# Retention projection of a decoder trunk: two heads as seven block products and two plain, or all four heads as seven block products with gates kept on the chip

## The chip, the core and the metric

The kernel runs on one core of one Trainium2 chip. Five engines with instruction streams of their own work side by side: TensorE (PE, with its weight loads as PEld), VectorE (DVE), ScalarE (ACT), GpSimd (POOL) and SyncE (SP). Each takes its instructions in the order in which they were written into its stream; semaphores hold an instruction until what it reads is there. Here SP and POOL mostly issue transfers between DRAM and SBUF. The metric is the device time of one execution in microseconds (us). All data are float32.

## The reference, cut to what matters

Two layers (DEPTH = 2) run over 512 tokens of width 1024. Each has a mixer (dilated attention beside retention), a residual with LayerNorm, and a SwiGLU feed-forward part. The change is in the mixer, from the point where both branches are there:

```
# _hybrid_mixer; y_a: 512 x 384 (attention), y_b: 512 x 2048 (retention, 4 heads x 512)
merged = (sigmoid(gate_a) * (y_a @ w_attn_proj)      # 384 x 1024
        + sigmoid(gate_b) * (y_b @ w_ret_proj))      # 2048 x 1024
return merged @ w_out                                # 1024 x 1024
```

`y_b @ w_ret_proj` is the **retention projection**, `y_a @ w_attn_proj` the attention projection, `merged @ w_out` the output projection.

## The kernel before

**Precision.** A float32 operand is split into a high and a low half of a shorter type (`hilo`): ACT casts the high half (L95), DVE subtracts it from the source for the low half (L96). A product is three matmuls (`mm3`): high by high, high by low, low by high. A matmul here takes a 128x128 token piece against 512 columns of weights, so a triple belongs to one k tile (128 rows of the weights) and one token tile (128 tokens). A `unit` is the split of one loaded 128x1024 weight tile: one cast, one subtraction. Its results come from pools of 4 `whi` and 4 `wlo` tiles; loaded tiles (`raw`) come from a pool of 8.

**Seven block products.** Where a product is written as 2 by 2 blocks, seven block products take the place of eight (`ORDER`, L313): A11·B11, A12·B21, S1·P1, S4·B22, S2·P2, S3·P3, A22·P4. A is the left side (tokens by k; first index the token half, second the k half), B the weights (k half, column half). The sums are S1 = A21−A22, S3 = A11−A21, S2 = S1−A11, S4 = S2+A12 on the left, and P1 = B11+B12, P2 = P1+B22, P4 = P2+B21, P3 = B12+B22 on the right. Some products add up in one PSUM pair (`CHAIN`), the rest is put together from PSUM by DVE.

**The mixer's end, in order of time** (in layer 0; layer 1 repeats it):

1. *Gates.* `gates(c)` computes the sigmoid gates. The attention gate stays in SBUF (`sga`), the retention gate goes from `sb` to DRAM (`g_d[1]`, L1113). The retention output y_b, transposed, is in DRAM (`y_d`). Near the end of the gates `y_blocks` loads four y blocks of heads 0 and 1 (`yr`, 128x4x256, L1092) on SP's queue.
2. *Attention projection* (L1145 to L1156): eight groups of nine matmuls. After each, DVE multiplies the gate by the product (L1153, 128x512) and POOL writes the result to `g_d[0]` (L1154). Between them stand ACT's and DVE's halves of y: `y_put` splits a block into `xh`, `xl`; `x_sums` (L213) forms S1, S3, S2, S4 on DVE and splits them into `xs`.
3. *Retention projection*: k tiles 0 to 7 (heads 0, 1) as seven block products (`product`: 7 x 4 k tiles x 2 token tiles), k tiles 8 to 15 (heads 2, 3) plainly (`plain`: 8 x 4 x 2 column halves). The seven products are interleaved with the two plain column halves. The weight sums grow in two tiles `p1`: SP loads B11, and POOL issues **adding DMAs** (transfers that add DRAM rows to what stands in SBUF; L1218) for B12, B22 and B21. A further pair gets B12 from SP and B22 by adding DMA (L1331). `yq_load` and `yq_put` bring the y of heads 2 and 3 (`yp`).
4. *Merging.* As results come out of PSUM, `gated` loads both gate products from `g_d` (512 KB each time), multiplies (L1252), adds (L1253), and puts a `turn` into the queue of side operations: four PE transposes (`px`, L1260), split into `m`.
5. *Output projection*, residual, norm.

**What sets the order.** The program is written in one order. Side operations stand in a list (`side`); `tick` pops one from it after so many microseconds' worth of matmuls. Within an engine the order is then fixed.

Of the kernel before, what the change touches and what calls it, by code (L numbers as in the profile page):

```python
# [55 lines left out]
def hybrid_kernel(ctx, tc, x, rel_bias, w_in, b_in, w_attn_proj, w_ret_proj, w_out,  # L56
# [457 lines left out]
    g_d = drp.tile([2, S, D], F32, name="g_d")  # L514
# [169 lines left out]
    def layer(ly, cp):  # L684
# [311 lines left out]
        with ret:  # L996
# [82 lines left out]
            sbp, sbs, yrs = [rp, 2], [], ExitStack()  # L1079
# [4 lines left out]

            def y_blocks():
                yas.close()
                ret.close()
                sbp[:] = lay.enter_context(stage("sbp")), 4
# [5 lines left out]
            def y_put(a, b):  # L1094
                ks, ts_ = slice(4 * b, 4 * b + 4), slice(a * 256, a * 256 + 256)
                hilo(yb[a][b], xh[:, ks, ts_], xl[:, ks, ts_])

            def gates(c):
# [10 lines left out]
                def right(i, t):  # L1109
                    sb = sbp[0].tile([P, S], F32, tag="sb", name="sb", bufs=sbp[1])  # L1110
                    sbs.append(sb)
                    act.activation(out=sb, in_=t, func=AF.Sigmoid)
                    act.dma_start(g_d[1, i * P:(i + 1) * P, cs], sb)  # L1113
# [11 lines left out]
            act.copy(out=xh[:, 0:8:4, 0:1], in_=sbs[-3][:, 0:2].unsqueeze(2))  # L1125

            def block_w(b, u):
                k = 4 * (b[1] == "2") + 2 * u
                c = (b[2] == "2") * S
                return wr_l[:, k:k + 2, c:c + S]  # L1130

            def plain_w(u, hf):
                return wr_l[:, 2 * RH + 2 * u:2 * RH + 2 * u + 2, hf * S:(hf + 1) * S]
# [25 lines left out]
        yrs.close()  # L1159

        fin = ExitStack()
        fp = fin.enter_context(stage("fin", side="right"))
        xt = [fp.tile([P, 2, D], F32, name="xtok")]
        res = (x if ly == 0 else spill).rearrange("(h i p) d -> h p i d", p=P, h=2)

# [34 lines left out]
        with stage("mp") as mp:  # L1200

            m = mp.tile([P, 2, KD, S], F32R, name="m")
            turns = [0] * NI
            rate[0], credit[0] = 0.5 / STEP, 0.0
            with stage("yp") as ypp, stage("pp", side="right") as ppp:
                pt = ppp.tile([P, 2, 2, S], F32, name="p1")
                p1 = [pt[:, u] for u in range(2)]
                yp = ypp.tile([P, 2, 6, S], F32R, name="yp")

                def y_tok(k, i):  # L1210
                    if k < 6:
                        return (yp[:, e, k, i * P:(i + 1) * P] for e in range(2))
                    ks, o = 2 * (k - 6) + i // 2, 256 + i % 2 * P
                    return (t[:, ks, o:o + P] for t in (xh, xl))

                def p_load(u, b, add):
                    if add:
                        pool.dma_start(p1[u], block_w(b, u), accum_op=ALU.add)  # L1218
                    else:
                        nc.sync.dma_start(p1[u], block_w(b, u))  # L1220

                def p_units():
                    return [unit(p1[u]) for u in range(2)]

                def product(an, units, pss, fresh):
                    ks = [(u, k) for u in units for k in range(2)]
                    for a in range(2):
                        for j, ((h, l), k) in enumerate(ks):
                            ah, al = x_left(an, j, slice(a * P, (a + 1) * P))
                            mm(pss[a], ah, h[:, k], fresh and j == 0, False)  # L1230
                            mm(pss[a], ah, l[:, k], False, False)
                            mm(pss[a], al, h[:, k], False, j == len(ks) - 1)
                            tick(STEP)

                def plain(u, unit_, pss):
                    h, l = unit_
                    for k in range(2):
                        for i in range(NI):
                            yh, yl = y_tok(2 * u + k, i)
                            mm(pss[i], yh, h[:, k], i >= 2 and u == 0 and k == 0, False)  # L1240
                            mm(pss[i], yh, l[:, k], False, False)
                            mm(pss[i], yl, h[:, k], False, u == 3 and k == 1)
                            tick(STEP)

                gv = {}

                def g_load(i, hf):
                    gv[i, hf] = load(g_d[:, i * P:(i + 1) * P, hf * S:(hf + 1) * S].rearrange("b p c -> p b c"), 2, S)

                def gated(i, hf, v):  # L1250
                    g = gv[i, hf]
                    dve.tensor_tensor(out=g[:, 1], in0=g[:, 1], in1=v, op=ALU.mult)  # L1252
                    dve.tensor_tensor(out=g[:, 0], in0=g[:, 0], in1=g[:, 1], op=ALU.add)  # L1253
                    turns[i] += 1

                    def turn():
                        turns[i] -= 1
                        px = psum()
                        for d in range(4):
                            pe.transpose(px[:, d * P:(d + 1) * P], g[:, 0, d * P:(d + 1) * P], ident)  # L1260
                        ks, ts_ = slice(4 * hf, 4 * hf + 4), slice(i * P, (i + 1) * P)
                        hilo(px.rearrange("p (d t) -> p d t", d=4), m[:, 0, ks, ts_], m[:, 1, ks, ts_])

                    side.extend([nothing] * (i % 2 == 0) * 2 + [turn])

                def pair():
                    return [psum("ps") for _ in range(2)]

                def copies(pss):
                    ts = [work("sn") for _ in pss]  # L1270
                    for t, ps in zip(ts, pss):
                        act.copy(out=t, in_=ps)
# [74 lines left out]
                for i in (2, 3):  # L1347
                    g_load(i, 1)
# [248 lines left out]
```

## Time and profile before

| what | value |
|---|---|
| median of 3 runs | 2100.8 us (2099.79 to 2102.8) |
| the profiled execution | 2106.83 us |
| its span (first to last instruction) | 2105.1 us, 33783 instructions |
| matmul records | 13178 |
| adding DMAs of L1218 and L1331, both layers | 16 |

The page gives busy time by engine, 40 slices of the span, the queues, the chain of work that ended last, and the costliest groups of instructions. A timeline row reads: start, duration, engine, line, operation, output <- inputs, shape; in brackets the idle time before it and what ended that. The durations of successive DVE or ACT rows overlap by a few hundredths, so what one instruction costs in a row of many is read from start to start. In layer 0 the attention projection's matmuls begin at 566.18 us and end at 582.50; the retention projection begins there and ends about 668.75. Layer 1 does the same 1043.5 us later (its attention projection begins at 1609.72 us).

### The profile page before, as it was taken

How to read it: one execution, taken by the hardware profiler on the slowest of the kernel's cores; microseconds unless marked ns; L12 is line 12 of the kernel's file. 1: busy time of each engine (PE TensorE's matmuls, PEld its weight loads, DVE VectorE, ACT ScalarE, POOL GpSimd, SP SyncE). 2: the span in 40 equal slices, each digit the busy share in tenths (PEclk: the TensorE clock that was granted, in tenths of full speed). 3: DMA queues.
4: the chain of work that ended last, by engine and by line, in shares of the span. 5: the costliest groups of instructions: out<-in, count | busy, mean ns of one | idle time of the engine just before them, and what ended most of it. 6: DMA issues, size and time to landing. Idle time of an engine off the chain costs nothing.

```text
span 2105.1 us, 33783 instructions
## 1 busy us (share of the span) xinstructions
PE 2084.9 (99%) x13178; PEld 1863.1 (89%) x13178; DVE 1622.4 (77%) x2327; ACT 1127.8 (54%) x1727; POOL 279.9 (13%) x288
## 2 busy tenths in 40 slices
PE   9999999999999999999999999999999999999998
PEld 8989888888878898999899898888888789989897
DVE  7666898786766698887787578887868577988876
ACT  5567655655643365555355766555656334655551
POOL 3111111110010101111030111111100111110101
PEclk9999999999999999999999999999999999999999
DMA  8866557676898458868258554758767973687771
GB/s 241 209 173 139 141 143 193 166 178 161 256 276 250 89 150 205 192 156 229 81 156 225 140 140 122 196 140 210 182 161 257 271 235 72 173 197 179 191 195 45
DMA packets 303553, 374.38 MB, mean 178 GB/s; under 512 B 22941, under 2 KB 208441, under 8 KB 303264
## 3 DMA queue, kind: packets, MB, share of 16 engines
q1 hardware_dynamic: 213056, 259.30, 40.0%
q0 software_dynamic: 62928, 100.11, 25.4%
q10 hardware_dynamic: 27408, 12.80, 2.1%
q8 instruction: 103, 1.69, 0.3%
q14 instruction: 58, 0.48, 0.1%
HBM read 346.30 MB, written 28.53 MB: 178 GB/s over the span
## 4 chain that ended last, share of the span: by engine, by line
PE 83%; DVE 5%; issue 5%; DMA 4%; ACT 2%; POOL 1%; ACTq 0%; SPq 0%; POOLq 0%; DVEq 0%
PE ps L84 74%; PE px L84 6%; DMA p<-in_w_ret_proj 2%; DMA raw<-in_w_in 1%; DVE wlo L351 1%; PE px L582 1%; ACT whi L345 1%; PE px L1044 1%; DVE wlo L96 1%; PE px L193 1%; DMA g_d<-sb 1%; DVE xs L96 0%; DVE sg L1153 0%; DVE yr L213 0%; PE px L1260 0%
## 5 line engine op out<-in xcount | busy, mean ns | idle before, releaser
L351 DVE TENSOR_TENSOR wlo<-raw,whi 128x1024 fp32r<-128x1024 f32 (+1 forms) x518 | 605.2, 1172 | 202.7 <-ACT whi L345 187.2
L345 ACT CAST whi<-raw 128x1024 fp32r<-128x1024 f32 (+1 forms) x518 | 519.5, 1007 | 451.0 <-PE ps L84 191.3
L84 PE MATMUL ps<-xs,whi 128*128 128x256 f32 x2176 | 399.5, 284 | 0.4 <-ACT sn L814 0.3
L84 PE MATMUL ps<-whi,xs 128*128 128x512 f32 (+1 forms) x1152 | 348.0, 372 | 2.1 <-ACT sn L496 2.1
L84 PEld LDWEIGHTS ps<-xs,whi 128*128 128x128 f32 x2176 | 339.5, 192 | 4.9 <-issue 1.7
L84 PE MATMUL ps<-xh,whi 128*128 128x256 f32 (+1 forms) x1104 | 318.3, 290 | 1.7 <-ACT xh L95 1.4
L84 PE MATMUL ps<-xl,whi 128*128 128x256 f32 (+1 forms) x1104 | 315.5, 286 | 0.0
L84 PE MATMUL ps<-xh,wlo 128*128 128x256 f32 (+1 forms) x1104 | 315.0, 286 | 0.0
L84 PE MATMUL ps<-xs,wlo 128*128 128x256 f32 x1088 | 308.0, 283 | 1.2 <-DVE wlo L351 1.2
L84 PEld LDWEIGHTS ps<-whi,xs 128*128 128x128 f32 x1152 | 210.0, 188 | 36.6 <-ACT sn L496 2.6
L84 PEld LDWEIGHTS ps<-xh,whi 128*128 128x128 f32 x1104 | 210.4, 191 | 9.6 <-ACT xh L95 2.8
L84 PEld LDWEIGHTS ps<-xl,whi 128*128 128x128 f32 x1104 | 211.4, 192 | 3.0 <-DVE xl L96 0.6
L84 PE MATMUL ps<-wlo,xs 128*128 128x512 f32 (+1 forms) x576 | 213.5, 371 | 0.4 <-DVE wlo L96 0.2
L84 PEld LDWEIGHTS ps<-xh,wlo 128*128 128x128 f32 x1104 | 211.2, 191 | 1.5
L84 PEld LDWEIGHTS ps<-xs,wlo 128*128 128x128 f32 x1088 | 208.5, 192 | 1.8 <-DVE wlo L351 1.8
L336 POOL DMA_DIRECT2D raw<-in_w_in x80 | 97.3, 1238 | 696.5 <-DMA raw<-in_w_in 204.8
L367 DVE TENSOR_TENSOR raw<-raw 128x1024 f32<-128x1024 f32 (+1 forms) x148 | 173.9, 1175 | 10.5 <-DMA raw<-in_w_in 8.5
L84 PE MATMUL ps<-whi,xh 128*128 128x512 f32 (+1 forms) x464 | 174.4, 376 | 0.0
L84 PE MATMUL ps<-whi,xl 128*128 128x512 f32 (+1 forms) x464 | 171.9, 370 | 0.0
L84 PE MATMUL ps<-wlo,xh 128*128 128x512 f32 (+1 forms) x464 | 171.8, 370 | 0.0
L84 PE MATMUL ps<-whi,ht 128*128 128x512 f32 x544 | 170.1, 390 | 0.0
L95 ACT CAST whi<-raw 128x1024 fp32r<-128x1024 f32 (+1 forms) x78 | 76.0, 984 | 100.5 <-PE ps L84 57.4
(247 smaller groups left out, 3307.7 us busy)
## 6 DMA issues: line engine op xcount, KB each, us to landing
raw<-in_w_in SPq DMA_DIRECT2D x168, 512.0 KB, 5.2
raw<-in_w_in POOLq DMA_DIRECT2D x64, 512.0 KB, 8.7
raw<-in_w_ffn_up SPq DMA_DIRECT2D x64, 512.0 KB, 5.0
raw<-in_w_ffn_down SPq DMA_DIRECT2D x52, 512.0 KB, 4.7
raw<-in_w_ffn_gate SPq DMA_DIRECT2D x44, 512.0 KB, 4.8
raw<-in_w_ffn_gate POOLq DMA_DIRECT2D x40, 512.0 KB, 7.3
raw<-in_w_ret_proj SPq DMA_DIRECT2D x32, 512.0 KB, 8.2
raw<-in_w_in SPq DMA_DIRECT2D x56, 256.0 KB, 4.9
```

The lines of the kernel that those rows point to most:

```text
L84: pe.matmul(ps, lhsT=a, rhs=b, start=start, stop=stop, skip_group_check=True)
L95: act.copy(out=hi, in_=src)
L96: dve.tensor_tensor(out=lo, in0=src, in1=hi.bitcast(F32), op=ALU.subtract)
L193: pe.transpose(px[:, d * P:(d + 1) * P], src[:, (4 * hf + d) * P:(4 * hf + d + 1) * P], ident)
L336: pool.dma_start(r, self.src({"P1": "B12", "P3": "B22"}[n], u), accum_op=ALU.add)
L345: act.copy(out=h, in_=src)
L351: dve.tensor_tensor(out=l, in0=src, in1=h.bitcast(F32), op=ALU.subtract)
L367: dve.tensor_tensor(out=r, in0=r, in1=self.t["B22" if n == "P2" else "B21", u], op=ALU.add)
L582: pe.transpose(px[:, hh, j * P:(j + 1) * P], ss[od][:, hh, j * P:(j + 1) * P], ident)
L1044: pe.transpose(px[:, t * P:(t + 1) * P], ys[i][:, t * P:(t + 1) * P], ident)
```

## The change

All 16 k tiles are now one set of seven block products: a block is 8 k tiles by 512 columns, in four units of two k tiles. The stream has 28 steps (`n`), four to a product (`g = n // 4`), each with 12 matmuls; `emit(n)` issues the conversion of a unit two steps ahead, and, behind it, the adding DMA or the load that follows in the same tile.

- **Weights.** Four raw tiles `pch` hold B11 and turn into P1, P2 and P4 in place by adding DMAs on POOL's queue (`add`, L1148). `b21` are loaded ahead; `b22` are loaded while product 1 (A12·B21) runs, and get B12 added in the tile (P3) once S4·B22 has used them. Per layer that is 16 adding DMAs on weights, where there were 8.
- **y.** Eight `yr` tiles, two to a block (L1097). S1 overwrites A22 (L1151), S3 overwrites A21 (L1155), S2 overwrites S1 (L1158). S4 = S2+A12 is formed by an adding DMA that adds A12 from DRAM to the tile of S2 (L1166, POOL's queue, two of them). A22 is loaded again into the tile of S3 (L1170, SP).
- **Gates.** The products of the attention gate stay in SBUF; the writes L1154 are gone, `g_d` holds the retention gate alone, and `gated` loads 256 KB each time. The sums go through `sga` (L1251).
- **Order.** Ahead of the first transposes stand four empty side operations (two before). Both `xtok` loads and the parameters of the norm are issued behind the last adding DMA on POOL.

The core of the diff, with the functions that the change adds:

```diff
@@ y blocks, attention projection
-                for a, b in ((0, 0), (0, 1), (1, 1), (1, 0)):
-                    yb[a][b] = yr.tile([P, 4, 256], F32, name=f"yr{a}{b}")
-                    nc.sync.dma_start(yb[a][b], y_v[:, 4 * b:4 * b + 4, a * 256:a * 256 + 256])
+                for a, b in ((0, 0), (1, 0), (1, 1), (0, 1)):
+                    yb[a][b] = [yr.tile([P, 4, 256], F32, tag=f"yr{a}{b}{u}", name="yr") for u in range(2)]
+                    for u in range(2):
+                        nc.sync.dma_start(yb[a][b][u], y_part(a, b, u))
...
-            b11, b21 = ([load(block_w(n, u), 2, S) for u in range(2)] for n in ("B11", "B21"))
-            for b in range(2):
-                y_put(0, b)
-            s1, s3, s2, s4 = x_sums(yb)
-            more = [lambda: y_put(1, 1), s1, s3, s2]
+            pch = [load(block_w("B11", u), 2, S) for u in range(4)]
+            b21 = [load(block_w("B21", u), 2, S) for u in range(4)]
+            def add(r, b, u):
+                pool.dma_start(r, block_w(b, u), accum_op=ALU.add)
+            def s1(u):
+                dve.scalar_tensor_tensor(out=a22[u], in0=a21[u], scalar=one, in1=a22[u], op0=ALU.mult, op1=ALU.subtract)
+                hilo(a22[u], xs[:, u, 0], xs[:, u, 1])
+            def s3_raw(u):
+                dve.tensor_tensor(out=a21[u], in0=a11[u], in1=a21[u], op=ALU.subtract)
+            def s2_raw(u):
+                dve.tensor_tensor(out=a22[u], in0=a22[u], in1=a11[u], op=ALU.subtract)
+            def s2_put(u):
+                for q in range(2):
+                    t = slot("s2")
+                    s2.append(t)
+                    h, l = (t[:, e].rearrange("p (k t) -> p k t", k=2) for e in range(2))
+                    hilo(a22[u][:, 2 * q:2 * q + 2], h, l)
+                pool.dma_start(a22[u], y_part(0, 1, u), accum_op=ALU.add)
+            def s3_put(u):
+                y_put(0, u, a21[u])
+                nc.sync.dma_start(a21[u], y_part(1, 1, u))
+            def s4_put(u):
+                hilo(a22[u], xs[:, 2 + u, 0], xs[:, 2 + u, 1])
+            for u in range(2):
+                y_put(0, u, a11[u])
+            for u in range(2):
+                y_put(256, u, a12[u])
+            more = [lambda f=f, u=u: f(u) for f in (s1, s3_raw, s2_raw, s2_put) for u in range(2)]
+            more += [nothing] * 2 + [lambda f=f, u=u: f(u) for f in (s3_put, s4_put) for u in range(2)]
+            more += [lambda u=u: y_put(256, u, a21[u]) for u in range(2)]
+            def emit(n):
+                g, u = divmod(n, 4)
+                if g in (0, 2, 4, 6):
+                    stream.append(unit(pch[u]))
+                    if g < 6:
+                        add(pch[u], ("B12", "B22", "B21")[g // 2], u)
+                elif g == 1:
+                    stream.append(unit(b21[u]))
+                    b22.append(load(block_w("B22", u), 2, S))
+                elif g in (3, 5):
+                    stream.append(unit(b22[u]))
+                    if g == 3:
+                        add(b22[u], "B12", u)
+                else:
+                    stream.append(unit(wo[u]))
+                if g in (5, 6):
+                    wo.append(load(wo_l[:, 2 * u:2 * u + 2, (g - 5) * S:(g - 4) * S], 2, S))
             for hf in range(2):
-                if hf:
-                    u11 = [unit(r) for r in b11]
                 for i in range(NI):
...
                     dve.tensor_tensor(out=v, in0=v, in1=ps, op=ALU.mult)
-                    pool.dma_start(g_d[0, i * P:(i + 1) * P, hf * S:(hf + 1) * S], v)
-                    if hf * NI + i >= 2 and more:
+                    if hf * NI + i >= 2:
                         more.pop(0)()
-            s4()
+                    if hf * NI + i in (5, 7):
+                        emit(len(stream))
@@ the stream (products and plain halves before)
+            for n in range(28):
+                g, u = divmod(n, 4)
+                i, an, _ = ORDER[g]
+                c = CHAIN[i]
+                emit(n + 2)
+                if more:
+                    more.pop(0)()
...
+                for k in range(2):
+                    for a in range(2):
+                        ah, al = y_left(an, 2 * u + k, slice(a * P, (a + 1) * P))
+                        p_ = pss[c][a]
+                        mm(p_, ah, h[:, k], i in FIRST and u == 0 and k == 0, False)
+                        mm(p_, ah, l[:, k], False, False)
+                        mm(p_, al, h[:, k], False, u == 3 and k == 1)
+                        tick(STEP)
```

The order of instructions shows three places. The first is DVE, from its first gate product to the low half of the first weight unit of A11·B11 (`wlo` of 128x1024, in the last row); `xl` and `xs` are low halves of y blocks and of their sums, the number behind a name tells buffers apart. Before:

```order
L1153 TENSOR_TENSOR sg_5355<-sg_5355,ps_6006 128x512
L96 TENSOR_TENSOR xl_80<-yr11_5883,xh_79 128x4x256
L1153 TENSOR_TENSOR sg_5386<-sg_5386,ps_6018 128x512
L213 TENSOR_TENSOR yr11_5883<-yr10_5885,yr11_5883 128x1024
L1153 TENSOR_TENSOR sg_5616<-sg_5616,ps_6030 128x512
L213 TENSOR_TENSOR yr10_5885<-yr00_5879,yr10_5885 128x1024
L96 TENSOR_TENSOR xs_81<-yr11_5883,xs_81 128x1024
L1153 TENSOR_TENSOR sg_5638<-sg_5638,ps_6044 128x512
L96 TENSOR_TENSOR wlo_6060<-raw_5994,whi_6059 128x1024
```

In the changed kernel the same stretch of DVE begins with a gate product, a first L1151 and a second gate product, and goes on:

```order
L1151 SCALAR_TENSOR_TENSOR yr_5888<-yr_5884,one_5979,yr_5888 128x1024
L1223 TENSOR_TENSOR sg_5616<-sg_5616,ps_6051 128x512
L96 TENSOR_TENSOR xl_80<-yr_5891,xh_79 128x4x256
L96 TENSOR_TENSOR xl_80<-yr_5892,xh_79 128x4x256
L96 TENSOR_TENSOR xs_81<-yr_5887,xs_81 128x1024
L1223 TENSOR_TENSOR sg_5638<-sg_5638,ps_6065 128x512
L96 TENSOR_TENSOR xs_81<-yr_5888,xs_81 128x1024
L1223 TENSOR_TENSOR sg_5355<-sg_5355,ps_6079 128x512
L1155 TENSOR_TENSOR yr_5883<-yr_5879,yr_5883 128x1024
L1223 TENSOR_TENSOR sg_5386<-sg_5386,ps_6091 128x512
L1155 TENSOR_TENSOR yr_5884<-yr_5880,yr_5884 128x1024
L96 TENSOR_TENSOR wlo_6104<-raw_6005,whi_6103 128x1024
```

Ahead of the first weight unit stood four gate products and four operations of 128x1024 before; now six gate products and eight operations of 128x1024 stand there. Between this unit and the second one stand two more gate products and two L1158 now, nothing before.

The second place is ACT in the products A11·B11 and A12·B21 of the changed kernel: `whi` are the high halves of weight units (the last two those of P1, from `raw_6005` and `raw_6007`), `xs` the high halves of S4, `sn` copies of the first product.

```order
L95 CAST whi_6227<-raw_6017 128x1024
L95 CAST xs_81<-yr_5887 128x1024
L1267 COPY sn_6223<-ps_6149 128x512
L1267 COPY sn_6224<-ps_6150 128x512
L95 CAST whi_6253<-raw_6019 128x1024
L95 CAST xh_79<-yr_5884 128x4x256
L95 CAST whi_6274<-raw_6005 128x1024
L95 CAST xs_81<-yr_5888 128x1024
L95 CAST whi_6297<-raw_6007 128x1024
```

Before, ACT had there:

```order
L95 CAST whi_6193<-raw_6149 128x1024
L95 CAST xs_81<-yr11_5883 128x1024
L1272 COPY sn_6198<-ps_6164 128x512
L95 CAST whi_6233<-raw_6231 128x1024
L95 CAST yp_6146<-raw_6151 128x1024
L95 CAST yp_6146<-raw_6229 128x1024
L95 CAST whi_6267<-raw_6265 128x1024
```

Both have a cast of S4 into `xs` ahead of weight units; now there are two of them, and what they read (`yr_5887`, `yr_5888`) is written by adding DMAs instead of by DVE.

The third place is POOL's transfers in this part of a layer. Before:

```order
L1154 DMA g_d<-sg 128x512 x8
L1342 DMA xtok<-in_x 128x2x1024
L1218 DMA p_6145<-in_w_ret_proj 128x2x512 x4
L1331 DMA raw<-in_w_ret_proj 128x2x512 x2
L1218 DMA p_6145<-in_w_ret_proj 128x2x512 x2
```

In the changed kernel:

```order
L1148 DMA raw<-in_w_ret_proj 128x2x512 x3
L1166 DMA yr<-y_d 128x4x256
L1148 DMA raw<-in_w_ret_proj 128x2x512
L1166 DMA yr<-y_d 128x4x256
L1148 DMA raw<-in_w_ret_proj 128x2x512 x12
L1329 DMA xtok<-in_x 128x2x1024 x2
```

The eight writes are gone, eight adding DMAs on weights and two on y have come, and the two on y stand behind three and four on weights.

More of the change, by code (lines that the diff above doesn't have):

```diff
@@ L1124, in layer @@
             drain()
-            act.copy(out=xh[:, 0:8:4, 0:1], in_=sbs[-3][:, 0:2].unsqueeze(2))
+            late = sbs[-3]
+            act.copy(out=xh[:, 0:8:4, 0:1], in_=late[:, 0:2].unsqueeze(2))
+            act.copy(out=xh[:, 0, 256:257], in_=late[:, 0:1])
+            one = sm.tile([P, 1], F32, tag="one", name="one", bufs=1)
+            dve.tensor_scalar(one, late[:, 0:1], 0.0, 1.0, op0=ALU.mult, op1=ALU.add)
             def block_w(b, u):
-                k = 4 * (b[1] == "2") + 2 * u
+                k = 8 * (b[1] == "2") + 2 * u
@@ new lines, in layer @@
+            for u in range(2):
[5 more added lines that the diff above has]
+            more += [lambda u=u: y_put(256, u, a21[u]) for u in range(2)]
+            wo_l = rows(w_out[ly])
+            b22, wo, stream = [], [], []
+            def emit(n):
[15 more added lines that the diff above has]
+                    wo.append(load(wo_l[:, 2 * u:2 * u + 2, (g - 5) * S:(g - 4) * S], 2, S))
@@ new lines, in layer, with g_load, g_slot, g_small @@
+            gv = {}
+            def g_load(hf, pair, ts):
+                for i, t in zip(pair, ts):
+                    gv[i, hf] = t
+                    nc.sync.dma_start(t, g_d[i * P:(i + 1) * P, hf * S:(hf + 1) * S])
+            def g_slot():
+                t = slot("gb", F32)
+                return [t[:, q] for q in range(2)]
+            def g_small():
+                return [sbp[0].tile([P, S], F32, tag="sb", name="gb", bufs=2) for _ in range(2)]
+            def gated(i, hf, v, o_=None):
+                g, ga = gv[i, hf], sga[i][:, hf]
+                if o_ is None:
+                    o_ = ga
+                dve.tensor_tensor(out=g, in0=g, in1=v, op=ALU.mult)
+                dve.tensor_tensor(out=o_, in0=ga, in1=g, op=ALU.add)
+                turns[i] += 1
+                def turn():
+                    turns[i] -= 1
+                    px = psum()
+                    for d in range(4):
+                        pe.transpose(px[:, d * P:(d + 1) * P], o_[:, d * P:(d + 1) * P], ident)
+                    ts_ = slice(i * P, (i + 1) * P)
+                    hilo(px.rearrange("p (d t) -> p d t", d=4), m[hf][:, 0, :, ts_], m[hf][:, 1, :, ts_])
+                side.extend([nothing] * (1 if i % 2 else 4) + [turn])
@@ L1158, in layer @@
+            emit(30)
+            emit(31)
         lay.close()
[L1159 removed]
         fin = ExitStack()
[L1162 to L1163 removed]
+        fp = fin.enter_context(stage("fin"))
+        xt = [fp.tile([P, 2, D], F32, tag=f"xtok{n}", name="xtok") for n in range(2)]
         res = (x if ly == 0 else spill).rearrange("(h i p) d -> h p i d", p=P, h=2)
+        for t, src in zip(xt, res):
+            pool.dma_start(t, src)
@@ new lines, in layer, with m_tok, evo @@
+        with stage("lp") as lp:
+            xc = [[lp.tile([P, 4, 256], F32, name=f"xc{a}{b}") for b in range(2)] for a in range(2)]
+            ln_par(lp.tile([P, 2 * D], F32, name="lnp"), ln1_g[ly], ln1_b[ly])
+            def m_tok(k, i):
+                return (m[k // 4][:, e, k % 4, i * P:(i + 1) * P] for e in range(2))
+            def evo(hf, i, ps):
+                residual(i, hf, ps, True, True)
+                if hf == 1:
+                    norm(i)
+                    side.extend([nothing] * (6, 2, 5, 4)[i] + to_xT(xtok(i), i, xc))
+            units = [stream[28:], tail_units(wo[4:])]
+            for hf, toks in ((0, (0, 1)), (1, (0,)), (1, (1,)), (0, (2, 3)), (1, (2,)), (1, (3,))):
+                while any(turns[i] for i in toks):
+                    side.popleft()()
+                xstat(units[hf], S, m_tok, lambda i, ps, hf=hf: evo(hf, i, ps), toks=toks)
```

241 lines of the change are left out of this document (66 added, 175 removed).

## Prediction

> **What bounds the kernel now.** I read the page's share of the engines first, then its chain of work that ended last, then the stretch that the change touches, by windows.
>
> ```profile
> PE 2084.9 (99%) x13178; PEld 1863.1 (89%) x13178; DVE 1622.4 (77%) x2327; ACT 1127.8 (54%) x1727; POOL 279.9 (13%) x288
> PE 83%; DVE 5%; issue 5%; DMA 4%; ACT 2%; POOL 1%; ACTq 0%; SPq 0%; POOLq 0%; DVEq 0%
> 566.18:582.50 16.32, 16.32 (x73) 13.51 (x72) 15.51 (x18) 8.63 (x11) 2.90 (x6) 1.00 0.92 335
> 582.50:593.38 10.88, 10.88 (x49) 9.01 (x48) 10.88 (x11) 10.30 (x13) 2.22 (x4) 1.00 0.78 265
> 593.38:640.00 46.62, 45.25 (x203) 36.88 (x202) 21.38 (x23) 14.23 (x19) 8.41 (x8) 1.00 1.00 276
> 640.00:668.75 28.75, 28.75 (x136) 23.75 (x135) 19.56 (x26) 10.87 (x13) 3.05 (x4) 1.00 0.74 218
> PE px L1260 <- DVE raw L1253: 1.3, 1, 1.3
> ```
>
> TensorE is the bound: busy 99% of the span. The windows are the attention projection, the first product A11·B11, and two pieces of the rest of the retention projection (columns: PE, PEld, DVE, ACT, POOL busy us with instructions, granted clock, DMA share, GB/s). The clock is 1.00 in all of them. But TensorE's margin is thin in its helpers: DVE has 15.51 of 16.32 us in the attention projection and all of 10.88 us in the first product, and the DMA engines are full (1.00) from 593.38 to 640.00. The last row (PE's waits between 550 and 740 us: total, times, longest) is the only wait of size there: 1.3 us for the first transposes. So fewer matmuls shorten the time one for one, and every us by which DVE or a transfer comes late lengthens it.
>
> **The matmuls removed.** The timeline of PE around 582 us:
>
> ```profile
> 582.50 0.39 PE L84 MATMUL ps<-whi,xh 128*128 128x512 f32 x1
> 582.73 0.39 PE L84 MATMUL ps<-wlo,xh 128*128 128x512 f32 x1
> 582.95 0.39 PE L84 MATMUL ps<-whi,xl 128*128 128x512 f32 x1
> ```
>
> One matmul costs 0.227 us (0.68 for a triple, start to start). Before, a layer has 7·4·2 triples for heads 0 and 1 and 8·4·2 for heads 2 and 3, 120 in all; now 7·8·2 = 112. 24 matmuls go: 24 x 0.227 = **−5.4 us per layer**, all on the path. The wait for the first transposes goes too, since four empty side operations stand ahead of them now: **−1.4** (the 1.3 above and about 0.1 behind it; if the copy of the other pair is late as well, 0).
>
> **What DVE must do before the first product.** Its timeline in the attention projection:
>
> ```profile
> 570.49 0.68 DVE L1153 TENSOR_TENSOR sg<-sg,ps 128x512 f32<-128x512 f32 x1
> 571.09 1.22 DVE L96 TENSOR_TENSOR xl<-yr,xh 128x1024 fp32r<-128x1024 f32 x1
> 572.22 0.68 DVE L1153 TENSOR_TENSOR sg<-sg,ps 128x512 f32<-128x512 f32 x1
> 572.82 1.22 DVE L213 TENSOR_TENSOR yr<-yr,yr 128x1024 f32<-128x1024 f32 x1
> 573.96 0.68 DVE L1153 TENSOR_TENSOR sg<-sg,ps 128x512 f32<-128x512 f32 x1
> L1183 DVE SCALAR_TENSOR_TENSOR xtok<-xtok,mv,lnp x16: 1272/1276/1278, 688.6 to 2098.1; 128x1024 f32<-128x1024 f32 x16
> ```
>
> Start to start a gate product costs 0.60 and any 128x1024 operation 1.14. (S1 is now a scalar_tensor_tensor; the nearest row is L1183 with 1.276 for the same size against 1.22, so I take the same.) From 570.49 on, the order has six gate products and eight operations of 128x1024 ahead of the first low half: 6·0.60 + 8·1.14 = 12.7 us, then 1.22 for itself. The eight y tiles are eight transfers of 0.524 MB; at the 335 GB/s of the first window that is 1.6 us each. The first landed when ACT's first `xh` started:
>
> ```profile
> 564.50 1.05 ACT L95 CAST xh<-yr 128x1024 fp32r<-128x1024 f32 x1 [2.82 <-DMA yr<-y_d]
> ```
>
> From there the eighth (A12) comes at 564.5 + 7·1.57 = 575.5, so A12's low halves hold DVE by about 1.1 us. The low half is there at 570.49 + 12.7 + 1.1 + 1.2 = 585.5; PE asks for it at 582.95 (two high products first). **+2.6** (with no wait for y and with 2.5 us of it: 1.5 and 4). Between this unit and the next stand two gate products and two operations of 128x1024: 585.5 + 2·0.60 + 2·1.14 + 1.2 = 590.1. PE has 14 matmuls to run by then, to 588.7: **+1.4** (0 to 2.1; nothing if ACT and DVE gain what they wait before). Before, the same work lay beside 192 plain matmuls and cost nothing.
>
> **S4 by an adding DMA.** This is the new wait. What an adding DMA takes here: the line that issues them, the timeline of ACT, and the queues between 613 and 623 us (packets, MB, share of 16 engines):
>
> ```profile
> DMA to landing us min/median/max: 5.5/7.6/11.7
> 610.56 1.05 ACT L95 CAST whi<-p 128x1024 fp32r<-128x1024 f32 x1 [15.27 <-DMA p<-in_w_ret_proj]
> 616.48 1.06 ACT L1272 COPY sn<-ps 128x512 f32<-128x512 f32 x2
> q0 software_dynamic: 536, 1.03, 67.5%
> q1 hardware_dynamic: 430, 0.83, 23.8%
> 601.30 1.23 POOL L1218 DMA_DIRECT2D p<-in_w_ret_proj  x1 [7.90 <-DMA p<-in_w_ret_proj]
> ```
>
> q0 is POOL's queue. Its 1.03 MB, two adds, had 67.5% of the 16 engines for 10 us: 3.4 us of all engines for each (a plain load of the same size: 23.8% of 10 us for 0.83 MB, 1.5 us). Issuing costs POOL 1.2 us. The adds on y have 1 KB rows, half as long as those on weights; no row shows that form, so I bound it by the weights' 3.4 below and, doubled with the rows, 6.8 above, and take 4.0, near the row. The first add on y can be issued when S2's halves are out and the third weight add is: about 592.5. The weight adds are issued as their tiles have been split, at 585.5, 590.2 and 591.4; queued one after another they land near 593, 596 and 599.4, and the y add, with loads of b22 beside it, at 604.2, 11.7 us after issue, which is the longest that the row above shows.
>
> [...]
>
> Behind the cast of S4 on ACT stand two copies of the first product and the last unit of B21, then the cast of P1's first unit. From 604.2: cast 1.05, copies 1.06, cast of the unit 1.05, its low half on DVE 1.2: 608.5. PE reaches that unit 68 matmuls after 590.1, at 605.5, and has one high product to run: **+2.8** (0 to 6: 0 where the add lands by 601.4, up to 8.9 us after issue, 6 where the longer form holds). The second add on y has one weight add ahead of it: at 4.0 each it lands at 612.3; cast of S4, cast and low half of P1's second unit, 615.8. PE comes there 24 matmuls after 608.5, at 614.0: **+1.8** (0 to 4). Then PE's first transposes, four empty operations behind the gated sums, want two gated results that DVE can make only behind the delayed low halves: five 128x512 and two 128x1024, 5.3 us after 615.8, at 621.1, against 619.5 by PE: **+1.6** (0 to 2).
>
> **What I cost at nothing.** The sixteen weight adds: each is issued eight steps (8·2.72 = 21.8 us) before its use. Four make 4·3.4 = 13.6 us of engine time per product of 10.9 us in the first three adding groups, so the cover shrinks by 3 us per group but does not run out (if it does: rival three). The eight writes that go and the halved gate loads free transfers that nobody waited for. The loads of w_out, `xtok` and the norm's parameters now come earlier or beside 20 us of matmuls. Six more weight units (28 for 22) and the extra y halves fill DVE where the third and fourth windows show it half to two thirds busy.
>
> **Sum.** Per layer −5.4 − 1.4 + 2.6 + 1.4 + 2.8 + 1.8 + 1.6 = +3.4; both layers have the same order, so **+6.8**. Against the profiled 2106.83 us (span 2105.1 and 1.7 around it) that is 2113.6; the profiled execution stands 6.0 above the median of the runs, so the runs' median would be 2100.8 + 6.8 = **2107.6 us**.
>
> **The rivals.**
>
> *The y adds land in time* (the other side: faster). Deciding point: an add lands by 601.4, at most 8.9 us after issue. The median of 7.6 speaks for it; that three weight adds stand ahead in the same queue speaks against. Then 2.8 and 1.8 go and 1.6 shrinks to about 0.4: −6.8 + 4.0 + 0.4 = −2.4 per layer, 2096. With DVE's lower bounds (1.5 and 0) it would be 2091.
>
> *Only one of the two adds is late.* Per layer −6.8 + 4.0 + 2 to 3 = about 0: 2101 to 2103.
>
> *The adds fall behind PE.* Twenty-eight steps last 76 us; sixteen weight adds and two on y take 18·3.4 = 61 us of all engines, the twelve plain loads of b22, wo 12·1.5 = 18: 79 us in all. If the queue does not run ahead at the start, PE waits in P2 and P4 too, by some 5 to 9 us per layer: 2118 to 2126. For it speaks that the DMA engines were full for 46 us before, with half the adds; against it that the writes are gone, and the loads of B11 and B21 are done before the stream.
>
> **How the numbers follow.** Forecast 0.44, y adds in time 0.28, one late 0.14, adds fall behind 0.14. The range takes most of the first rival and half of the last: 2093 to 2121. A measurement of this kernel can tell about 0.2% (4.2 us) from no change: faster is below 2096.6, slower above 2105.0. Faster: somewhat over half of the first rival and little else, 0.20. Same: the rest of it, the second, and the forecast's low end, 0.34. Slower: 0.46.
>
> **What would show it.** In the profile after: 48 fewer matmuls; PE idle some 2.6 us before the second matmul of A11·B11, released by DVE `wlo`; ACT's `xs` cast waiting for a DMA on `yr` from `y_d`, and PE some 23 us into the projection waiting for a `whi` or `wlo` behind it; the y add's time to landing near 11 us. No such wait of ACT, or adds that land in under 9 us, would make the first rival true; waits for weight units in the last four products would make the third true. The prediction would be wrong altogether if DVE were found to run ahead in the attention projection by starting S1 earlier, or if POOL issued its adds later than reckoned.

## The result, and the profile after

| | us |
|---|---|
| before, median of 6 runs | 2102.4 (2099.8 to 2104.5) |
| changed, median of 6 runs | 2119.9 (2116.6 to 2122.8) |
| ratio, 95% interval | 1.0084 (1.0071 to 1.0097) |
| profiled execution, span | 2121.81, 2120.0 |

The change costs 17.5 us. The forecast was slower by 6.8, with a range from 2093 to 2121: the direction held, and the time lies near the range's upper end; the size forecast was less than half. First the page and TensorE's four longest waits between 550 and 740 us (total, times, longest) in the changed kernel, then windows of layer 0 from the first matmul of the attention projection to the first of the output projection (columns as before).

```profile
PE 2083.3 (98%) x13130; PEld 1855.4 (88%) x13130; DVE 1644.6 (78%) x2347; ACT 1146.2 (54%) x1747; POOL 297.2 (14%) x292
PE 82%; issue 8%; DMA 3%; DVE 3%; ACT 2%; POOL 1%; ACTq 0%; POOLq 0%; DVEq 0%
PE ps L84 <- DVE wlo L96: 3.5, 2, 2.6
PE ps L84 <- DVE sn L1314: 3.0, 1, 3.0
PE ps L84 <- ACT whi L95: 2.0, 2, 1.3
PE px L1258 <- DVE sg L1251: 1.1, 1, 1.1
566.71:583.03 16.32, 16.32 (x74) 13.52 (x73) 14.01 (x15) 9.15 (x11) 0.00 (x0) 1.00 1.06 374
583.03:593.91 10.88, 7.60 (x25) 5.49 (x24) 10.88 (x13) 4.78 (x7) 3.96 (x4) 0.84 0.54 114
593.91:640.53 46.62, 42.94 (x188) 34.07 (x187) 32.02 (x33) 23.82 (x27) 16.71 (x14) 1.00 1.10 230
640.53:677.77 37.24, 34.28 (x150) 27.50 (x149) 27.80 (x32) 18.75 (x21) 1.20 (x1) 0.95 0.87 246
```

The 48 matmuls are gone (13178 to 13130). In the four windows that the forecast shows for the same stages TensorE was busy through 101.20 of 102.57 us; now it is busy through 101.14 of 111.06. It pauses in three of four windows, and in two of them the granted clock is below 1 (0.84 and 0.95). Where the time went is best read as the length of the retention projection, from the start of the attention projection's last matmul to that of the output projection's first: 86.5 us in layer 0 and 86.6 in layer 1 before, **95.0 and 91.9** now (582.80 to 677.77 and 1634.85 to 1726.73), 13.7 us more in all. The spans differ by 14.9; the remaining 1.2 lies outside these two stretches.

The pauses one by one, on the engines that end them. In the timelines of DVE and of ACT in the changed kernel:

```profile
582.10 1.22 DVE L1155 TENSOR_TENSOR yr<-yr 128x1024 f32<-128x1024 f32 x1
583.24 0.68 DVE L1223 TENSOR_TENSOR sg<-sg,ps 128x512 f32<-128x512 f32 x1
583.83 1.22 DVE L1155 TENSOR_TENSOR yr<-yr 128x1024 f32<-128x1024 f32 x1
584.97 1.22 DVE L96 TENSOR_TENSOR wlo<-raw,whi 128x1024 fp32r<-128x1024 f32 x1
603.77 1.05 ACT L95 CAST xs<-yr 128x1024 fp32r<-128x1024 f32 x1 [5.40 <-DMA yr<-y_d]
612.79 1.05 ACT L95 CAST xs<-yr 128x1024 fp32r<-128x1024 f32 x1 [4.16 <-DMA yr<-y_d]
660.56 1.05 ACT L95 CAST xs<-raw 128x1024 fp32r<-128x1024 f32 x1 [1.43 <-DMA raw<-in_w_out]
661.64 1.23 DVE L96 TENSOR_TENSOR xs<-raw,xs 128x1024 fp32r<-128x1024 f32 x1 [1.25 <-ACT xs L95]
662.78 0.68 DVE L96 TENSOR_TENSOR m<-px,m 128x512 fp32r<-128x512 f32 x1
663.38 1.27 DVE L1314 TENSOR_TENSOR sn<-sn,ps 128x512 f32<-128x512 f32 x2
```

DVE makes the first low half at 584.97 to 586.19, behind S3; the casts of S4 wait for the y adds until 603.77 and 612.79 (forecast 604.2 and 612.3). The third group was not foreseen. A11·B11, S2·P2 and S3·P3 add up in one PSUM pair. After S3·P3, DVE must read this chain (L1314) before A22·P4 may add to it, and that reading stands behind a conversion of the output projection's weights into `xs`, which had waited for its cast and the cast for its load. In kernel.py this conversion is written behind L1314 (`tail_units`, L1378); on DVE it stands ahead of it, so the order in which the program is written does not tell this one. In layer 1 DVE has the same order: its first reading ends at about 1714.6, and TensorE goes on at 1714.77. The profile puts that wait down to a cast of ACT that ended within 0.1 us of the reading; experiment 3 shows that it is the same wait. TensorE's own rows, at the first pause and at that one:

```profile
583.03 0.61 PE L84 MATMUL ps<-whi,xh 128*128 128x512 f32 x2
586.24 0.50 PE L84 MATMUL ps<-wlo,xh 128*128 128x512 f32 x1 [2.60 <-DVE wlo L96]
587.59 0.63 PE L84 MATMUL ps<-whi,xh 128*128 128x512 f32 x1
588.01 0.63 PE L84 MATMUL ps<-wlo,xh 128*128 128x512 f32 x1
660.85 0.40 PE L84 MATMUL ps<-whi,xl 128*128 128x512 f32 x1
664.21 0.47 PE L84 MATMUL ps<-whi,xh 128*128 128x512 f32 x1 [2.96 <-DVE sn L1314]
666.33 0.63 PE L84 MATMUL ps<-wlo,xh 128*128 128x512 f32 x1
666.75 0.63 PE L84 MATMUL ps<-whi,xl 128*128 128x512 f32 x1
```

About a microsecond after each of these two pauses matmuls start 0.43 us apart instead of 0.227, seven of them in each case: 1.4 us on top of the pause. So these two pauses, 2.99 and 3.36 us from start to start, cost 4.2 and 4.5 us.

### The profile page after: what moved, and what is told of

The parts are those of the page before. It is cut to its first block, busy times and chain, and to the rows that moved or that the text cites. A ratio compares the mean times of both kernels' runs of the same rounds, so it can differ in the third digit from the quotient of the medians.

```text
span 2120.0 us, 33718 instructions
## 1 busy us (share of the span) xinstructions
PE 2083.3 (98%) x13130; PEld 1855.4 (88%) x13130; DVE 1644.6 (78%) x2347; ACT 1146.2 (54%) x1747; POOL 297.2 (14%) x292
## 4 chain that ended last, share of the span: by engine, by line
PE 82%; issue 8%; DMA 3%; DVE 3%; ACT 2%; POOL 1%; ACTq 0%; POOLq 0%; DVEq 0%
PE ps L84 73%; PE px L84 7%; DMA yr<-y_d 2%; DMA raw<-in_w_in 1%; PE px L582 1%; DVE wlo L351 1%; PE px L1044 1%; ACT whi L345 1%; PE px L193 1%; DMA raw<-in_w_out 0%; DVE wlo L96 0%; DMA raw<-in_w_ret_proj 0%; ACT whi L95 0%; POOL ry L135 0%; DVE raw L363 0%
## 5 line engine op out<-in xcount | busy, mean ns | idle before, releaser
L345 ACT CAST whi<-raw 128x1024 fp32r<-128x1024 f32 (+1 forms) x518 | 519.7, 1008 | 452.3 <-PE ps L84 189.8
L351 DVE TENSOR_TENSOR wlo<-raw,whi 128x1024 fp32r<-128x1024 f32 (+1 forms) x518 | 604.9, 1172 | 204.3 <-ACT whi L345 189.0
L84 PE MATMUL ps<-whi,xh 128*128 128x512 f32 (+1 forms) x512 | 193.9, 381 | 6.8 <-ACT whi L95 3.9
L84 PE MATMUL ps<-wlo,xh 128*128 128x512 f32 (+1 forms) x512 | 192.3, 376 | 4.5 <-DVE wlo L96 4.3
L84 PE MATMUL ps<-whi,xl 128*128 128x512 f32 (+1 forms) x512 | 192.2, 375 | 0.0
L96 DVE TENSOR_TENSOR wlo<-raw,whi 128x1024 fp32r<-128x1024 f32 (+1 forms) x102 | 117.2, 1158 | 53.6 <-ACT whi L95 53.6
```

The source lines that it names most:

```text
L84: pe.matmul(ps, lhsT=a, rhs=b, start=start, stop=stop, skip_group_check=True)
L96: dve.tensor_tensor(out=lo, in0=src, in1=hi.bitcast(F32), op=ALU.subtract)
L345: act.copy(out=h, in_=src)
L351: dve.tensor_tensor(out=l, in0=src, in1=h.bitcast(F32), op=ALU.subtract)
```

## The experiments

Ratios are to the kernel before, with 95% intervals; "retention" is the length defined above, layer 0 and layer 1, from each kernel's trace.

| kernel | ratio | retention, us |
|---|---|---|
| changed | 1.0084 (1.0071 to 1.0097) | 95.0, 91.9 |
| 1 S4 by DVE | 1.0015 (1.0006 to 1.0024) | 91.2, 87.9 |
| 2 units early | 1.0081 (1.0067 to 1.0094) | 95.7, 94.2 |
| 3 tail conversions late | 1.0040 (1.0026 to 1.0053) | 93.8, 90.4 |
| 4 all three | 0.9979 (0.9970 to 0.9988) | 84.8, 83.7 |
| 5 sums on POOL | 1.0016 (1.0007 to 1.0025) | 88.1, 87.3 |
| 7 gate writes back | 1.0087 (1.0069 to 1.0104) | 96.3, 97.1 |
| 8 y one tile earlier | 0.9951 (0.9937 to 0.9964) | 80.8, 80.8 |
| 9 y two tiles earlier | 0.9951 (0.9938 to 0.9963) | 80.8, 81.3 |
| 10 only y earlier | 1.0072 (1.0058 to 1.0086) | 93.4, 93.6 |
| 11 as 8, adding DMAs kept | 1.0021 (1.0012 to 1.0030) | 88.9, 88.0 |
| 12 bank by bank | 0.9947 (0.9933 to 0.9961) | 80.1, 80.1 |

The theory was that three waits make up the loss (DVE's work ahead of the first units; the y adds; the conversions ahead of L1314), each with its own cause. The rival: the weight adds or DVE's total load set the pace, and taking one wait away only moves it.

**1. S4 by DVE.** A12 is still in SBUF, so the sum needs no transfer.

```diff
-                pool.dma_start(a22[u], y_part(0, 1, u), accum_op=ALU.add)
+                dve.tensor_tensor(out=a22[u], in0=a22[u], in1=a12[u], op=ALU.add)
```

> S4 = S2 + A12 is formed by two DVE additions of 128x1024 from the A12 tiles that are still in SBUF, instead of by the two adding DMAs; all else as in the changed kernel. Theory 1 (the casts of S4 wait for the adding DMAs and hold weight units behind them on ACT): the waits of TensorE 23 to 42 us into the retention projection (0.4 + 2.8 + 1.4 + 0.5 us in layer 0, about the same in layer 1) go, the wait of 3 us before the second matmul stays: about 2110 us, 10 less than the changed kernel. Theory 2 (sixteen weight adds fill POOL's queue, so the weight units would be late in any case): TensorE waits there for casts of P1 instead, at least 2 us per layer: 2116 to 2120.

The waits for the y adds and for the transposes are gone, and no new ones came in their place; two that stay grew (in layer 0 from 3.0 to 3.9 us at the first low half and from 3.4 to 3.7 at L1314, from start to start, and in layer 1 from 2.8 to 3.1 at L1314, now with slow matmuls behind it). The retention projection is 3.8 and 4.0 us shorter. The ratio falls by 0.7%, some 14 us, which is more than these 7.7 and than the 9.1 by which the traced spans differ; what the rest is stays open. Sixteen weight adds run in time; theory 2 falls.

**2. Units early.**

```diff
-                    if hf * NI + i in (5, 7):
+                    if hf * NI + i in (4, 5):
                         emit(len(stream))
```

> The first two weight units of A11.B11 are converted one and two token tiles earlier, ahead of the second half of S3 and of S2; nothing else is written differently. Theory 1 (DVE's order ahead of the first unit): the wait of 3.0 us, the half clock behind it and the wait for the second unit (5.4 us in layer 0, 3.2 in layer 1) go; TensorE then comes to the y adds 4 to 5 us earlier, so about half is given back there: 2113 to 2117. If the y adds did not bind: 2111. Rival (DVE is short of time altogether, the place of the unit is nothing): the same us are lost at the next units: 2119 or more.

No gain, where theory 1 had 2113 to 2117: the time is the rival's. The first pause shrinks (2.3 and 1.1 us from start to start, for 3.0 and 2.1), but TensorE then comes earlier to the y adds and waits there longer (2.2 and 1.3 us in a row in layer 0, 3.2 and 1.3 in layer 1), and slow matmuls follow. The causes stand in series: while the y adds bind, DVE's order is worth nothing.

**3. Tail conversions late.** The `xs` conversions are queued behind the last transposed halves; `turned_` holds the two instructions that `turn` made last.

```diff
-            units = [stream[28:], tail_units(wo[4:])]
+            with tc.issue_after(turned_[0].ins), tc.issue_after(turned_[1].ins):
+                units = [stream[28:], tail_units(wo[4:])]
```

> The conversions of the output projection's second-half weights (four casts and four subtractions into xs) are queued behind the last transposed halves on ACT and DVE; else as the changed kernel. Theory 1 (DVE reads the chain of products 1, 6, 7 from PSUM behind such a conversion, which waits for its load, and A22.P4 waits for that reading): the wait of 3.0 us after S3.P3 shrinks to about 1 in both layers, and the half clock behind it in layer 0 (1.6 us) goes: about 2115. Rival (both PSUM banks end in the same step, so the reading is late whatever stands ahead): 2.5 us stay per layer, the clock too: 2118 to 2120.

TensorE's waits of this kernel between 640 and 690 us:

```profile
PE ps L84 <- DVE sn L1314: 0.7, 1, 0.7
```

The wait fell from 3.0 to 0.7 (from start to start 3.4 to 1.1 in layer 0 and 2.8 to 1.1 in layer 1), and no slow matmuls follow it. The retention projection got 1.1 and 1.5 us shorter only, since other pauses before it grew (3.8 from start to start at the first low half in layer 0, for 3.0); the ratio fell by 0.44%, with intervals of 0.13% to each side. That is more than these 2.6 us explain: the span is 5.5 us shorter, half of it in stretches that the edit leaves alone.

**4. All three edits.**

> The three edits together: S4 by DVE, first two units early, tail conversions late. Theory 1 (these three waits are all of the loss): the 48 matmuls that went (10.9 us) and the old wait for the transposes (2.8) are left as gain, with 1 to 2 us of waits per layer: 2090 to 2094, against 2102.4 for the kernel before. Theory 2 (the weight adds or DVE's total load bind next): 2100 or more, with new waits for whi or wlo in P1, P2 or P4.

Faster than before now, but by 0.2%, not the 0.5% expected. Windows of DVE's busiest stretch in layer 0, this kernel:

```profile
540.00:570.00 30.00, 30.00 (x134) 24.85 (x133) 19.81 (x22) 16.39 (x24) 0.00 (x0) 1.00 0.72 236
570.00:580.30 10.30, 10.30 (x47) 8.55 (x46) 9.41 (x11) 6.39 (x7) 0.00 (x0) 1.00 1.06 374
580.30:613.00 32.70, 29.81 (x129) 23.45 (x129) 32.70 (x36) 20.77 (x24) 8.17 (x7) 1.00 0.93 213
```

From 580.3 to 613.0 DVE is busy all 32.70 us, and TensorE 29.81: DVE is the bound there once the waits are gone. From 540 to 570 it has 10 us free. Here the rival is right about DVE's load. Two ways to relieve it follow.

**5. Sums on POOL.** With the three edits of experiment 4, S3 and S4 by `pool.tensor_tensor` in place of `dve.tensor_tensor`.

> As the kernel with all three edits, but S3 = A11 - A21 and S4 = S2 + A12 (four operations of 128x1024 per layer) are made by POOL instead of DVE. Theory 1 (with the three waits gone DVE is the bound: busy 32.7 of 32.7 us from 580.3 to 613.0): 4.6 us of DVE work per layer go, so the waits for wlo (3.5 us in layer 0, 2.3 in layer 1) nearly vanish: 2 to 3 us less per layer, about 4 to 6 us below that kernel, a ratio near 0.9955 to the kernel before. Rival (POOL is slow at this size and its weight adds stand behind these operations, or DVE slows beside it): no gain or a loss, ratio 0.998 or more.

Slower than the kernel without it by 0.4%. Rows of POOL and of DVE in this kernel:

```profile
572.23 2.40 POOL L1155 TENSOR_TENSOR yr<-yr 128x1024 f32<-128x1024 f32 x1 [41.97 <-DMA yr<-y_d]
592.71 6.78 POOL L1166 TENSOR_TENSOR yr<-yr 128x1024 f32<-128x1024 f32 x1
572.61 3.11 DVE L1151 SCALAR_TENSOR_TENSOR yr<-yr,one 128x1024 f32<-128x1024 f32 x1
576.24 4.24 DVE L96 TENSOR_TENSOR xl<-yr,xh 128x1024 fp32r<-128x1024 f32 x2
601.55 2.60 DVE L96 TENSOR_TENSOR wlo<-raw,whi 128x1024 fp32r<-128x1024 f32 x1 [4.32 <-ACT whi L95]
```

While POOL makes S3 in 2.40 us, DVE's operation takes 3.11 instead of 1.28; beside the second S3 (2.41 us from 575.85) two subtractions take 4.24 instead of 2.35. Later POOL's row is the long one: S4, of the same size, takes 6.78 us at 592.71, beside operations of DVE that keep their length (1.21 and 1.28). Beside the second S4 (2.85 us from 600.21) it is DVE again, with 2.60 for 1.21. In each of these four overlaps one engine took longer, and the time shows no relief: the ratio is 1.0016, where experiment 4 has 0.9979.

**6. Idle work on DVE** ahead of the first unit, on top of experiment 4, to see what a pause costs (the results of the added operations are not used).

```diff
-                    if hf * NI + i in (4, 5):
+                    if hf * NI + i == 4:
+                        z = work("z")
+                        for _ in range((2, 6)[ly]):
+                            zi = dve.tensor_tensor(out=z, in0=v, in1=v, op=ALU.add)
+                        with tc.issue_after(zi.ins):
+                            emit(len(stream))
+                    if hf * NI + i == 5:
                         emit(len(stream))
```

> As the kernel with all three edits, with idle work on DVE (additions of 128x512 whose result nobody reads: two in layer 0, six in layer 1) ahead of the first weight unit of A11.B11. Theory (TensorE halves its rate after a pause of about 3 us or more): the pause at the second matmul grows from 1.8 to about 3.0 us in layer 0 and from 0.8 to about 4.4 in layer 1; behind it 5 to 12 matmuls stand 0.43 us apart instead of 0.227 in layer 1, and perhaps in layer 0, 1.0 to 2.4 us more. Rival (the slow matmuls come from weights that are late, not from the pause): matmuls 0.227 apart behind both pauses.

One run: 2109.4 us, beside 2105.5 for the kernel before. Layer 1 of its trace, TensorE:

```profile
1624.44 0.61 PE L84 MATMUL ps<-whi,xh 128*128 128x512 f32 x2
1633.09 0.79 PE L84 MATMUL ps<-wlo,xh 128*128 128x512 f32 x1 [8.03 <-DVE wlo L96]
1633.68 0.63 PE L84 MATMUL ps<-whi,xl 128*128 128x512 f32 x1
1635.81 0.63 PE L84 MATMUL ps<-whi,xl 128*128 128x512 f32 x1
1636.50 0.39 PE L84 MATMUL ps<-wlo,xh 128*128 128x512 f32 x1
```

The pause was longer than meant (8 us, since five more of DVE's operations came to stand ahead of the unit). Behind it matmuls stood 0.43 apart for about 3 us, as behind the pause of 3.2 us in layer 0. TensorE waits for nothing in either slow stretch, so weights that come late are not its reason; it came behind the pause in both layers, and after 8.4 us it was no more than after 3.2.

**7. Gate writes back**, to a place in DRAM that nobody reads.

```diff
                     dve.tensor_tensor(out=v, in0=v, in1=ps, op=ALU.mult)
+                    pool.dma_start(ga_d[i * P:(i + 1) * P, hf * S:(hf + 1) * S], v)
```

> The changed kernel with the eight writes of attention gate products to DRAM put back (256 KB each, POOL's queue, behind each gate product); nobody reads them. Theory 1 (these transfers were hidden before, and their removal is worth nothing): 2118 to 2122, as the changed kernel. Rival (they compete with the y tiles and the weights, 2.1 MB at some 340 GB/s, and stand ahead of the weight adds on POOL): the first unit's wait grows by 2 us or more per layer: 2124 or more.

1.0087 against 1.0084: no difference that these runs can tell. The median, 2125.4 us, lies where the rival had it, but the kernel before was 3.1 us slower in these runs too, so the ratio decides. The retention projection of its one trace is longer (96.3 and 97.1), with longer waits behind the y adds (3.9 and 1.3 us in a row in layer 1), so a cost of a few us is not ruled out. Keeping the gates in SBUF did not cause the loss.

**8 and 9. The y loads earlier.** With the three edits of experiment 4:

```diff
-                if n_ == 2:
+                if n_ == 1:
```

(0 in experiment 9).

> As the kernel with all three edits, with the loads of the eight y tiles issued one token tile of the second gate half earlier. Theory 1 (DVE is the bound from 580 to 613 us, and half idle between 540 and 570): four to five of DVE's operations on y move ahead of the attention projection's first gate product, some 5 us of DVE work; the waits for wlo (3.5 us in layer 0, 2.3 in layer 1) go almost wholly: 5 to 6 us below that kernel, a ratio to the kernel before of about 0.995. Rival (the loads collide with the last transfers of the gates' weights, or hold DVE and ACT in order ahead of the attention projection's units): no gain, 0.998 or more, with a new wait at the attention projection's start.

> The same with the loads two token tiles earlier. Theory 1: no more than one tile earlier gives, 0.994 to 0.996, since DVE's work on y cannot start before the gates let go of xh; rival (loads compete with the gates' own weights): slower than one tile earlier, 0.997 or more.

Both 0.9951, as forecast from DVE's load. The same windows as in experiment 4, and all of TensorE's waits between 530 and 670 us, in experiment 8:

```profile
540.00:570.00 30.00, 30.00 (x134) 24.84 (x133) 23.87 (x25) 19.98 (x29) 0.00 (x0) 1.00 0.96 335
580.30:613.00 32.70, 32.70 (x148) 27.07 (x147) 31.66 (x34) 21.64 (x26) 8.38 (x7) 1.00 1.02 241
...
PE ps L84 <- DVE sn L1314: 0.7, 1, 0.7
```

Four us of DVE's work moved into the stretch where it was idle for a third of the time (19.81 to 23.87 of 30), and TensorE is busy throughout both windows.

**10 and 11. What the y adds cost then.** Experiment 10 is the changed kernel with the earlier loads alone; 11 is experiment 8 with the adding DMAs for S4 put back.

> The changed kernel with the y loads one token tile earlier and nothing else: S4 by adding DMAs, units and tail conversions as they were. Theory 1 (three causes beside each other; DVE's work ahead of the first unit is only one): the wait at the second matmul goes, the y adds are issued some 5 us earlier but TensorE comes 5 us earlier too, so 5 to 8 us of waits for them stay per layer, and the 3 us after S3.P3: ratio 1.002 to 1.007. Rival (all waits were one chain that began with DVE's lateness): they go as well, 0.996 to 0.998.

> The kernel with the three edits and the earlier y loads, but S4 formed by the two adding DMAs again. Its difference to that kernel (0.9951) is the price of the adding DMAs when DVE is not late. Theory 1: they still take 10 us or more from issue to landing behind weight adds in one queue, and hold weight units on ACT: 4 to 7 us per layer, ratio 0.999 to 1.002. Rival (issued early enough they land in time): 0.995 to 0.996.

10 stays at 1.0072, 11 is 0.7% slower than 8 (8.0 and 7.2 us more per retention projection). The y adds in 11, from issue to landing (least, median, most), and ACT's wait for two of them:

```profile
DMA to landing us min/median/max: 9.7/13.3/16.6
ACT xs L95 <- DMA yr<-y_d: 12.1, 2, 7.0
```

Measured from the start of the attention projection, the first is issued 4.2 us earlier than in the changed kernel and lands 4.3 us earlier; TensorE, held by nothing ahead, comes 5 us earlier. They bind whether DVE is late or not: the forecast's rival, that they land in time, is refuted by the changed kernel and by both of these.

**12. Bank by bank.** Experiment 8, with the matmuls of one PSUM bank ahead of the other's in the two steps on both sides of L1314.

```diff
-                for k in range(2):
-                    for a in range(2):
+                pairs = [(k, a) for k in range(2) for a in range(2)]
+                for k, a in sorted(pairs, key=lambda q: q[1]) if n in (23, 24) else pairs:
```

> The kernel with the three edits and the earlier y loads, and in the last step of S3.P3 and the first of A22.P4 the matmuls of one PSUM bank stand before those of the other. Theory: the first bank is complete 1.36 us earlier and the second asked for 1.36 us later, so the last wait (0.86 us per layer, for DVE's reading of the chain) goes: 1.7 us less, ratio about 0.9943. Rival (DVE is busy with the transposed halves then): the wait stays, 0.995.

The trace shows no wait of TensorE between 560 and 680 us any more, and the projection takes 80.1 us in both layers, 0.8 less than in 8. The ratio, 0.9947, cannot be told from 0.9951. This version has the lowest median of all, 2091.9 us (experiment 8: 2093.6).

## Why the forecast had the direction right and the size wrong

Point by point, layer 0 and layer 1, from starts of matmuls in the changed kernel (pause less the 0.23 of an undisturbed one):

| term | forecast | measured |
|---|---|---|
| 24 matmuls fewer | −5.4 | −5.4 (48 records fewer) |
| first low half late | +2.6 | +2.8, +1.9 |
| second unit | +1.4 | +0.9, +1.0 |
| last unit of B21 behind S4 | +2.8 | +0.3, +0.2 |
| P1's second unit behind S4 | +1.8 | +2.7, +3.1 |
| first transposes | +1.6 | +1.3, +1.3 |
| old wait for transposes gone | −1.4 | −1.5, −1.5 |
| reading the chain before A22·P4 | 0 | +3.1, +2.5 |
| matmuls at half rate | 0 | +2.8, 0 |

The table's sums are 7.0 and 3.1 us; the measured 8.5 and 5.2 hold smaller pauses of 0.1 to 0.7 us beside these.

- *The matmuls.* Right, and shown apart from the rest: experiment 12 has the same matmuls as the changed kernel and no waits, and its retention projection is 6.4 and 6.6 us shorter than before, 5.4 for the matmuls and the rest for the old waits.
- *DVE ahead of the first unit.* Right: from the order and two durations, 585.5 was forecast for the end of the low half; it was 586.2, with an attention projection that starts 0.5 us later in this trace.
- *S4 by adding DMA.* Right that it binds. Counted from the start of the attention projection, the two adds landed 1.0 and 0.1 us earlier than forecast in layer 0, and 3.0 and 1.7 earlier in layer 1. The term sized wrongly is where the first one meets TensorE (+2.8 forecast, +0.3 and +0.2 measured): in layer 0 TensorE came 1.5 us later than forecast, held by the slow matmuls behind the first pause, and in layer 1 it was the add that came 3.0 us early. So the first add was nearly in time, and the second was not. Experiments 1 and 11 give its price as it stands: 3.8 and 4.0 us in the changed kernel, 8.0 and 7.2 where nothing else is late.
- *"What I cost at nothing."* This is the step that failed. The loads of w_out were put down as earlier or beside 20 us of matmuls; their conversions were not placed in DVE's order at all. One of them stood ahead of L1314. Experiment 3 shows it (3.0 to 0.7 us). The forecast had looked at who waits for the changed operations, not at what now stands ahead of an old one; and it did not ask how far apart PSUM's two banks end: before, all matmuls of one token tile came ahead of the other's, now they alternate. Experiment 12 shows that part (0.7 to nothing).
- *The price of a pause.* A pause was counted at its length. In layer 0 two of 3 us brought seven slow matmuls each, 2.8 us in all.
- *The eight writes.* Counted at nothing, and nothing measurable came of putting them back.
- *The rivals.* The third (weight adds fall behind) is refuted: with nothing else late (8, 12) all sixteen are in time. The first read its chance from the adds of L1218 alone; the four of L1331 took 10.5 to 13.4 us in the same trace of the kernel before, which spoke against it. The second rival's sum, −6.8 + 4.0 + 2 to 3, is −0.8 to +0.2 per layer, 2099 to 2101, not 2101 to 2103.

Added up, the two unforeseen terms are 5.9 us in layer 0 and 2.5 in layer 1, 8.4 of the 13.7 us. The foreseen ones, as measured, come to 1.1 and 0.6: 1.7 us where 6.8 was forecast, and less than the 4.2 from which the forecast calls a kernel slower. So the direction came out right in good part by luck, through terms that the sum did not have. Experiment 3, which takes most of one of them away, stays slower (1.0040), but with longer pauses elsewhere.

## What to carry to other kernels

When a change lets an engine that sets the bound run ahead, list for every instruction that it waits for what stands ahead of it on its own engine, the work of the next stage included; waits stand in series, and undoing one alone may show little (experiments 2 and 10). The two adding DMAs on y took a median of 13.2 us from issue to landing in the changed kernel, 16.8 at most, so one like them is cheap only where nobody waits within that time: for a sum whose inputs are already in SBUF, the 1.14 us that an operation of this size took on DVE is less. And before giving DVE more work, find the stretch in which it is idle and load its inputs there.

## What the runs showed of the hardware

- **Some pauses cost more than their length.** In layer 0 of the changed kernel the pauses of 2.99 and 3.36 us between starts of matmuls each brought seven matmuls at 0.43 us for 0.227, 1.4 us; in layer 1 single pauses of 2.10 and 2.77 us brought none. In the retention projections of all traces of this study, single pauses of up to 2.2 us left at most one slow matmul; of those from 2.3 to 2.9 us some brought six or seven and some none (2.83 none, 2.31 and 2.80 did); each from 3.0 us on brought five to ten, 1.0 to 2.0 us. After 8.4 us (experiment 6, layer 1) six stood 0.43 apart, no more than after 3.36. Two shorter pauses close together sometimes did it too (1.10 and 1.45 us in experiment 3, 1.30 and 1.45 in experiment 7), and sometimes not (1.67 and 1.45 in the changed kernel). In the windows 588 to 590 and 666 to 668 us of the changed kernel, within its two slow stretches, the granted clock is 0.50. By what rule a pause brings them is not shown.
- **Adding DMAs with 1 KB rows** took 9.0 to 16.8 us from issue to landing in the changed kernel (median 13.2), those on weights with 2 KB rows 5.3 to 13.2 (median 8.1). In one queue, with loads beside them, a y add landed 3.0 to 5.4 us behind the one ahead of it. That the shorter rows are the reason is not shown: the weight add between the two y adds took 13.2 and 12.0 us and landed 4.0 us behind.
- **Some operations of DVE and POOL on 128x1024 took longer side by side** (experiment 5): beside POOL's S3 of 2.40 us DVE's half of S1 took 3.11 us, where the half before it took 1.28; beside POOL's second S4 of 2.85 us one took 2.60, for 1.21. POOL's first S4 took 6.78 us beside operations of DVE that kept their length. What POOL takes at this size with DVE idle was not measured.
